# A first sum of activations moved from GpSimd to VectorE, and a norm's statistics from VectorE to ScalarE, in a streaming encoder step

## The chip, the cores and the metric

The kernel runs on one core of one Trainium2 chip. The metric is device time in microseconds (us) for one execution of the whole step, the median over repeated runs. Engines are named as in the profile: PE (TensorE matmul), PEld (its weight load), DVE (VectorE), ACT (ScalarE), POOL (GpSimd), SP (SyncE, which issues most DMAs).

## The reference

One layer is computed for 2048 prompt frames and 64 sample frames, D_MODEL = 1024, D_FF = 2816. The change lies in the last two lines of the layer, the SwiGLU and the last norm:

```
def _post(x, mix, ln1_g, ln1_b, w_gate_up, w_down, ln2_g, ln2_b):
    h = _layernorm(ALPHA * x + mix, ln1_g, ln1_b)
    gu = h @ w_gate_up
    f = (jax.nn.silu(gu[..., :D_FF]) * gu[..., D_FF:]) @ w_down
    return _layernorm(ALPHA * h + f, ln2_g, ln2_b)
```

## The kernel before

**Blocks and positions.** The frames are cut into four blocks b of 576, 512, 512 and 512 tokens; a block has four token tiles t of 128 rows (the first has a fifth of 64 rows). For each block the kernel goes over 22 slices i of 128 gate and up columns. The two matrix products of a slice are made by a seven-product scheme: products 1, 5, 6, 2, 7, 4, 3, each 12 fp32r matmuls of 256 columns (four pieces of K, three matmuls each for high and low parts, lines 909 to 911). `order` lists all products; the place of one in that list is its position. At each position the program writes the product, and then every step that was booked for that position with `at`. All queues run in the order in which the program is written; waits between engines are semaphores that follow from the data.

**Banks.** Products 1, 6, 7 and 4 of a slice add up one after another in the same PSUM bank A. Between them ScalarE copies the bank out (`keep`, line 915), and the next of them can't start before that copy. Product 2 has bank S1 (bankS in the profile), 5 and 3 bank C. VectorE adds the copies to other banks (lines 919, 946); ScalarE takes the silu (lines 950, 958).

**Chunks.** Two slices (2c and 2c+1) make a chunk c. In blocks 1 to 3, for chunks 2 to 9 (2 to 8 in block 3), which are 23 in all, the down product too is made by a seven-product scheme (`strassen`). There `out` multiplies silu and up into a tile g (line 926), two of them for a chunk (x and y in `f_sums`, each with two halves of 128x256), and `f_sums` makes four sums and differences of them on GpSimd at line 879, in the order of products 5, 7, 6, 3, in place. `put_hi` rounds such a sum on ScalarE (line 886, the high part) and `put_lo` subtracts that on VectorE (line 890, the low part). `unit(b, c, prod, u)` then makes one half of one product on PE: three matmuls of 512 columns at lines 1333, 1334, 1335, of which the third alone needs the low part; VectorE adds its bank to y (line 1338).

With p0 the position of product 3 of slice 2c+1, unit (5, 0) stands at p0 + 5, (6, 0) at p0 + 6; the high parts of 5, 6, 3, 7 at p0 + 3, 4, 5, 6 and the low parts one position later. The split of a gate/up weight slice, too, runs partly on GpSimd (line 113, wf<-guraw), and in some chunks GpSimd subtracts pieces of h for the next block (line 747, hsum and hraw).

**Where blocks meet.** The last chunk of a block ends within the first 20 positions of the next. For tile k of the block the two halves h of the down product stand at p0 + 10 + 2k and + 11 + 2k (line 1292 adds them to y), and the steps of `finish_steps` at + 2k + 11, 12, 13, 15, 17: statistics of half 0 (bn_stats, line 1354), of half 1 with mean and variance (line 1347) and 1/sqrt (line 91 and a small GpSimd instruction, line 92), gain (line 1367), shift (line 1371), store. In the first block all this is two positions later. There are 5 + 4 + 4 = 13 such tiles; the last block has its own ending, in which the statistics of three of its four tiles are already made from ScalarE's accumulated sums (`z_sum`, `z_mean`, `z_sq`, `z_var`, lines 1409 to 1425).

Of the kernel before, what the change touches and what calls it, by code (L numbers as in the profile page):

```python
# [16 lines left out]
P = 128  # L17
D = 1024
# [27 lines left out]
def hybrid_step(ctx: ExitStack, tc: tile.TileContext, x_prompt, x_sample, xT_prompt, xT_sample, cache_kT, cache_v, w_in,  # L46
# [824 lines left out]
        f = ffs[b, c, prod] = half_form()  # L871
        split(f[:, 0], f[:, 1], src)

    def f_sums(b, c):

        x, y = g_t.pop((b, 2 * c)), g_t.pop((b, 2 * c + 1))
        for prod, o, a, d, op in ((5, y[:, 1], x[:, 1], y[:, 1], ALU.add), (7, x[:, 1], x[:, 0], x[:, 1], ALU.subtract),
                                  (6, x[:, 0], y[:, 1], x[:, 0], ALU.subtract), (3, y[:, 0], y[:, 0], x[:, 0], ALU.subtract)):
            nc.gpsimd.tensor_tensor(out=o, in0=a, in1=d, op=op)
        for prod, o in ((5, y[:, 1]), (6, x[:, 0]), (7, x[:, 1]), (3, y[:, 0])):  # L880
            f_sum[b, c, prod] = o

    def put_hi(b, c, prod):

# [12 lines left out]
    def product(b, i, prod):  # L897
        n = TB[b] // 2
        w, h = wf.pop((b, i, prod)), forms[b, prod]
        bk = {1: "A", 6: "A", 7: "A", 4: "A", 2: "B", 5: "C", 3: "C"}[prod]  # L900
        new = prod in (1, 2, 5)
        if new:
            acc[i, bk] = (bank({"A": f"A{i % 2}", "C": f"C{i % 2}", "B": "S1"}[bk]) if b else
                          ps1.tile([P, 512], F32, name=f"acc{bk}", tag="x", bufs=6))
        ps = acc[i, bk][:, :n]
        for k in range(4):
            wh, wl, hh, hl = w[:, 0, k], w[:, 1, k], h[:, 0, k, :n], h[:, 1, k, :n]

            nc.tensor.matmul(ps, wh, hh, start=(new and k == 0), stop=False, skip_group_check=not new)  # L909
            nc.tensor.matmul(ps, wh, hl, start=False, stop=False, skip_group_check=not new)  # L910
            nc.tensor.matmul(ps, wl, hh, start=False, stop=(k == 3), skip_group_check=not new)  # L911

        def keep(key):
            part[i, key] = tmp(key)
            nc.scalar.copy(part[i, key][:, :n], ps)  # L915

        def add(key, to):
            part[i, key] = a = part.pop((i, to))
            nc.vector.tensor_tensor(out=a[:, :n], in0=ps, in1=a[:, :n], op=ALU.add)  # L919

        def out(sh, g, u):
            if strassen(b, i):
                if sh == 0:
                    g_t[b, i] = f2.tile([P, 4, P], F32, name="g", tag="wsum", bufs=3).rearrange("p (s a) q -> p s (a q)", s=2)
                to = g_t[b, i][:, sh]
                nc.vector.tensor_tensor(out=to, in0=u, in1=g, op=ALU.mult)

                if not (sh and i % 2 == 0):
                    put_f(b, i // 2, 4 if sh else 1 + i % 2, to)
                if sh and i % 2:  # L930
                    f_sums(b, i // 2)
                return
            nc.vector.tensor_tensor(out=g, in0=u, in1=g, op=ALU.mult)
            f = ff[b, i][:, :, sh * n:(sh + 1) * n] if b == 0 else half_form()
            if b:
                ff[b, i, sh] = f
            split(f[:, 0], f[:, 1], g)

        if prod == 1:
            keep("a0")  # L940
        elif prod == 6:
            keep("a1")
        elif prod == 7:
            keep("a2")
            part[i, "c22"] = a = part.pop((i, "a2"))
            nc.vector.tensor_tensor(out=a[:, :n], in0=acc[i, "C"][:, :n], in1=a[:, :n], op=ALU.add)
        elif prod == 2:
            add("c11", "a0")
            g = part[i, "c11"][:, :n]
            nc.scalar.activation(g, g, AF.Silu)  # L950
        elif prod == 4:
            if b == 0:
                ff[b, i] = f2.tile([P, 4 * NHX], F32R, name="ff", tag="ff", bufs=4)[:, :4 * n].rearrange("p (s t) -> p s t", s=2)
            out(0, part.pop((i, "c11"))[:, :n], ps)
        elif prod == 3:
            add("c12", "a1")
            g = part.pop((i, "c12"))[:, :n]
            nc.scalar.activation(g, g, AF.Silu)  # L958
            out(1, g, part.pop((i, "c22"))[:, :n])
# [399 lines left out]
    def finish_steps(t):  # L1359

        s_, m = {}, rows(t)

        def z(h):
            return y_t[t][:, h * 512:(h + 1) * 512]

        def gain():
            nc.vector.scalar_tensor_tensor(out=y_t[t][:m], in0=y_t[t][:m], scalar=s_["mv"][:m, 0:1], in1=ln2g[:m],
                                           op0=ALU.subtract, op1=ALU.mult)

        def shift():  # L1370
            nc.vector.scalar_tensor_tensor(out=y_t[t][:m], in0=y_t[t][:m], scalar=s_["rs"][:m, 0:1], in1=ln2b[:m],
                                           op0=ALU.mult, op1=ALU.add)

        def out():
            nc.sync.dma_start(out=y_out(t), in_=y_t.pop(t)[:m])

        return [lambda: stats(s_, (z(0), z(1)), m, 0), lambda: (stats(s_, (z(0), z(1)), m, 1), moments(s_, m)),
                gain, shift, out]


    zs, zp, zm = {}, {}, {}
# [71 lines left out]
    for b in range(NB):  # L1453
        first, last = b * NO, b == NB - 1
        for c in range(NFF // 2):
            p0 = start[b, 2 * c + 1, 3]
            d_load, d_split = (-8, -1, -5, -3), (-3, 5, -1, 4)
            if strassen(b, 2 * c):
                for prod, q0, q1 in ((1, -6, -3), (2, -5, -2), (5, -2, 2), (6, -1, 3), (3, 1, 5), (7, 4, 7), (4, 6, 9)):
                    at(p0 + q0, lambda b=b, c=c, prod=prod: load_f(b, c, prod))  # L1460
                    at(p0 + q1, lambda b=b, c=c, prod=prod: split_hi(b, c, prod))
                    at(p0 + q1 + 1, lambda b=b, c=c, prod=prod: split_lo(b, c, prod))
                for q, prod, u in ((0, 1, 0), (1, 2, 0), (2, 1, 1), (3, 2, 1), (5, 5, 0), (6, 6, 0), (7, 5, 1), (8, 3, 0), (8, 6, 1),
                                   (9, 3, 1), (10, 7, 0), (11, 7, 1), (12, 4, 0), (13, 4, 1)):
                    at(p0 + q, lambda b=b, c=c, prod=prod, u=u: unit(b, c, prod, u))
                for q, prod in ((3, 5), (4, 6), (5, 3), (6, 7)):
                    at(p0 + q, lambda b=b, c=c, prod=prod: put_hi(b, c, prod))
                    at(p0 + q + 1, lambda b=b, c=c, prod=prod: put_lo(b, c, prod))
                continue
# [25 lines left out]
            elif not last:  # L1495
# [4 lines left out]
                for k, t in enumerate(TILES[b]):  # L1500
                    for h in range(2):
                        at(p0 + 10 + 2 * k + (h if b else 2 - h), lambda b=b, c=c, t=t, h=h: down(b, c, t, h))
                    steps = finish_steps(t)
                    for q, f in zip((11, 12, 13, 15, 17), steps):
                        at(p0 + 2 * k + q + late, f)
                    at(p0 + 2 * k + 20 + late, lambda t=new.pop(0): new_y(t)) if new else None
        if not last:
# [106 lines left out]
```

## Time and profile before

| | us |
|---|---|
| median of 3 runs (2204.99 to 2209.4) | 2208.36 |
| the profiled execution, its own time | 2207.18 |
| its span, first to last instruction | 2205.4 |
| PE busy | 2089.7 (95%) |
| DVE busy | 1640.3 (74%) |
| ACT busy | 997.0 (45%) |
| POOL busy | 702.2 (32%) |

The profile is of one execution; a row of the time line gives an instruction's start in us from the span's start, its duration, engine, line, and in brackets how long the engine had been idle and who released it. A busy PE isn't a PE at its peak, so the reading goes by the places where PE is idle, and by who ended that idle time.

### The profile page before, as it was taken

The page shows a single profiled execution, that of the slowest core. Times are in us where ns is not written, and L with a number is a line of the kernel's source. Part 1 is how long each engine was busy: PE and PEld are TensorE (multiplying, and loading weights), DVE is VectorE, ACT ScalarE, POOL GpSimd, SP SyncE. Part 2 cuts the span into 40 slices and gives each one's busy share as a digit, 9 for nine tenths or more (in the row PEclk, how much of TensorE's full clock was granted, in tenths as well). Part 3 has the DMA queues.
Part 4 walks back from the last instruction along what each step waited for, and adds up shares of the span by engine and source line. Part 5 has one row for each costly group of instructions (what it writes and reads, how often), then busy time and mean ns, then how long its engine had stood idle before and what let it go on. Part 6 is the DMA issues. An engine that isn't in the chain of part 4 may idle for free.

```text
span 2205.4 us, 36220 instructions
## 1 busy us (share of the span) xinstructions
PE 2089.7 (95%) x13081; PEld 1861.6 (84%) x13081; DVE 1640.3 (74%) x3176; ACT 997.0 (45%) x2385; POOL 702.2 (32%) x644
## 2 busy tenths in 40 slices
PE   8999999989989899999999999999999999999997
PEld 6888888867768799999888888888888888988986
DVE  6877777786788677777786776777677778577775
ACT  6666666563343444444433443453343444344443
POOL 0222222231132567666531332222243222122221
PEclk9999999989999999999999999999999999999999
DMA  5111111043554866676776767787587777767663
GB/s 196 39 39 39 39 39 39 27 159 118 196 193 172 306 231 235 247 285 241 273 278 240 257 238 277 264 285 278 199 287 273 251 257 276 257 225 262 242 230 121
DMA packets 189156, 447.22 MB, mean 203 GB/s; under 512 B 22608, under 2 KB 53072, under 8 KB 188976
## 3 DMA queue, kind: packets, MB, share of 16 engines
q1 hardware_dynamic: 168432, 426.22, 54.9%
q10 hardware_dynamic: 20368, 18.35, 2.5%
q8 instruction: 103, 1.69, 0.3%
q14 instruction: 77, 0.63, 0.1%
q0 software_dynamic: 176, 0.33, 0.0%
HBM read 345.94 MB, written 98.89 MB: 202 GB/s over the span
## 4 chain that ended last, share of the span: by engine, by line
PE 65%; DVE 20%; ACT 6%; DMA 4%; issue 3%; POOL 1%; ACTq 0%; SPq 0%; DVEq 0%; POOLq 0%
PE bankA L909 5%; PE bankA L911 4%; PE bankA L910 4%; PE pj L158 2%; PE pj L159 2%; PE pj L160 2%; PE bankC L910 2%; PE bankC L909 2%; PE bankC L911 2%; PE pd L159 2%; PE pd L160 2%; PE pd L158 2%; PE bankD L1334 2%; PE bankD L1333 2%; PE bankD L1335 2%
## 5 line engine op out<-in xcount | busy, mean ns | idle before, releaser
L113 POOL TENSOR_TENSOR wf<-guraw,wf 128x512 fp32r<-128x512 f32 x173 | 245.7, 1420 | 626.9 <-ACT wf L112 598.4
L909 PE MATMUL bankA<-hf,wf 128*128 128x256 f32 x1056 | 301.8, 286 | 12.2 <-ACT a L915 11.9
L910 PE MATMUL bankA<-hf,wf 128*128 128x256 f32 x1056 | 300.1, 284 | 0.0
L911 PE MATMUL bankA<-hf,wf 128*128 128x256 f32 x1056 | 299.9, 284 | 0.0
L909 PEld LDWEIGHTS bankA<-hf,wf 128*128 128x128 f32 x1056 | 201.4, 191 | 22.7 <-ACT a L915 14.6
L910 PEld LDWEIGHTS bankA<-hf,wf 128*128 128x128 f32 x1056 | 201.2, 191 | 9.1
L911 PEld LDWEIGHTS bankA<-hf,wf 128*128 128x128 f32 x1056 | 201.4, 191 | 0.0
L112 ACT CAST wf<-guraw 128x512 fp32r<-128x512 f32 x264 | 163.1, 618 | 19.7 <-DMA guraw<-in_w_gate_up_dram 12.6
L915 ACT COPY a<-bankA 128x256 f32<-128x256 f32 x198 | 73.5, 371 | 174.8 <-PE bankA L911 174.4
L910 PE MATMUL bankC<-hf,wf 128*128 128x256 f32 x528 | 149.4, 283 | 2.6 <-DVE hf L113 2.6
L909 PE MATMUL bankC<-hf,wf 128*128 128x256 f32 x528 | 149.8, 284 | 0.9 <-DMA wf<-wf_d 0.8
L911 PE MATMUL bankC<-hf,wf 128*128 128x256 f32 x528 | 148.5, 281 | 0.0
L1338 DVE TENSOR_TENSOR y<-bankD,y 128x512 f32<-128x512 f32 x184 | 125.6, 683 | 30.5 <-PE bankD L1335 30.5
L1326 DVE TENSOR_TENSOR wd<-draw,wd 128x512 fp32r<-128x512 f32 x161 | 130.8, 813 | 0.0
L950 ACT ACTIVATE a<-a 128x256 f32<-128x256 f32 (+1 forms) x88 | 37.4, 425 | 200.7 <-DVE a L919 199.7
L909 PE MATMUL accA<-hf,wf 128*128 128x288 f32 x352 | 105.2, 299 | 8.9 <-ACT a L915 5.3
L958 ACT ACTIVATE a<-a 128x256 f32<-128x256 f32 (+1 forms) x88 | 37.4, 424 | 155.9 <-DVE a L919 155.8
L910 PEld LDWEIGHTS bankC<-hf,wf 128*128 128x128 f32 x528 | 99.5, 188 | 8.6 <-DVE hf L113 3.2
L1338 DVE TENSOR_TENSOR y<-bankS,y 128x512 f32<-128x512 f32 x138 | 94.4, 684 | 16.1 <-PE bankS L1335 13.7
L909 PEld LDWEIGHTS bankC<-hf,wf 128*128 128x128 f32 x528 | 99.8, 189 | 7.0 <-DMA wf<-wf_d 1.4
L911 PE MATMUL accA<-hf,wf 128*128 128x288 f32 x352 | 104.1, 296 | 0.4 <-DVE wf L113 0.4
L910 PE MATMUL accA<-hf,wf 128*128 128x288 f32 x352 | 104.4, 297 | 0.0
(336 smaller groups left out, 6712.1 us busy)
## 6 DMA issues: line engine op xcount, KB each, us to landing
wf<-wf_d SPq DMA_DIRECT2D x264, 512.0 KB, 4.9
guraw<-in_w_gate_up_dram SPq DMA_DIRECT2D x110, 512.0 KB, 6.2
wf_d<-wf SPq DMA_DIRECT2D x88, 512.0 KB, 4.9
draw<-in_w_down_dram SPq DMA_DIRECT2D x153, 256.0 KB, 3.5
draw<-wt_d SPq DMA_DIRECT2D x92, 256.0 KB, 4.3
guraw<-in_w_gate_up_dram SPq DMA_DIRECT2D x66, 256.0 KB, 6.4
wt_d<-draw SPq DMA_DIRECT2D x44, 256.0 KB, 3.3
hraw<-h_d SPq DMA_DIRECT2D x42, 256.0 KB, 4.7
```

What stands on the lines that cost most here:

```text
L112: nc.scalar.copy(hi, src)
L113: (on or nc.vector).tensor_tensor(out=lo, in0=src, in1=hi.bitcast(F32), op=ALU.subtract)
L158: nc.tensor.matmul(out, ah, bh, start=(i == 0), stop=False)
L159: nc.tensor.matmul(out, ah, bl, start=False, stop=False)
L160: nc.tensor.matmul(out, al, bh, start=False, stop=(i == n - 1))
L909: nc.tensor.matmul(ps, wh, hh, start=(new and k == 0), stop=False, skip_group_check=not new)
L910: nc.tensor.matmul(ps, wh, hl, start=False, stop=False, skip_group_check=not new)
L911: nc.tensor.matmul(ps, wl, hh, start=False, stop=(k == 3), skip_group_check=not new)
L915: nc.scalar.copy(part[i, key][:, :n], ps)
L1326: nc.vector.tensor_tensor(out=hl[:, 1], in0=d_raw.pop((b, c, "f", prod)), in1=hl[:, 0].bitcast(F32), op=ALU.subtract)
L1333: nc.tensor.matmul(pd, fh, w[:, 0], start=new, stop=False, skip_group_check=not new)
L1338: nc.vector.tensor_tensor(out=y, in0=pd, in1=y, op=ALU.add)
```

## The change

**In the 23 chunks**, the first sum of `f_sums` (that for product 5) is made on VectorE in `out`, right behind the multiplication that completes its inputs and ahead of the split of product 4. It goes into u, the buffer of the up half that was just read, in place of the tile's own half. GpSimd keeps three subtractions; the one for product 6 reads the new sum. The high part of 5 moves from p0 + 3 to p0 + 2, its low part from p0 + 4 to p0 + 3.

**Where blocks meet**, bn_stats and bn_aggr of 13 tiles go. ScalarE copies each half of y onto itself with an accumulated sum, VectorE makes minus the mean from the two sums, ScalarE squares y minus mean with an accumulated sum for each half, and VectorE makes the variance from these two. Variance and gain together stand at + 2k + 14, one position later than the gain stood; shift and store stay.

```
-    def f_sums(b, c):
+    def f_sums(b, c, first):
         x, y = g_t.pop((b, 2 * c)), g_t.pop((b, 2 * c + 1))
-        for prod, o, a, d, op in ((5, y[:, 1], x[:, 1], y[:, 1], ALU.add), (7, x[:, 1], x[:, 0], x[:, 1], ALU.subtract),
-                                  (6, x[:, 0], y[:, 1], x[:, 0], ALU.subtract), (3, y[:, 0], y[:, 0], x[:, 0], ALU.subtract)):
-            nc.gpsimd.tensor_tensor(out=o, in0=a, in1=d, op=op)
-        for prod, o in ((5, y[:, 1]), (6, x[:, 0]), (7, x[:, 1]), (3, y[:, 0])):
+        for prod, o, a, d in ((7, x[:, 1], x[:, 0], x[:, 1]), (6, x[:, 0], first, x[:, 0]), (3, y[:, 0], y[:, 0], x[:, 0])):
+            nc.gpsimd.tensor_tensor(out=o, in0=a, in1=d, op=ALU.subtract)
             f_sum[b, c, prod] = o
+        f_sum[b, c, 5] = first
...
                 nc.vector.tensor_tensor(out=to, in0=u, in1=g, op=ALU.mult)
+                if sh and i % 2:
+                    nc.vector.tensor_tensor(out=u, in0=g_t[b, i - 1][:, 1], in1=to, op=ALU.add)
...
                 if sh and i % 2:
-                    f_sums(b, i // 2)
+                    f_sums(b, i // 2, u)
...
+        def total(h):
+            if h == 0:
+                s_.update({x: f2.tile([P, 2], F32, name=f"y{x}", tag=f"z{x}", bufs=3) for x in ("sum", "sq", "mv", "rs")})
+            nc.scalar.activation(z(h)[:m], z(h)[:m], AF.Copy, accum_out=s_["sum"][:m, h:h + 1])
+        def squares():
+            nc.vector.tensor_scalar(s_["mv"][:m, 0:1], s_["sum"][:m, 0:1], s_["sum"][:m, 1:2], -1.0 / D, op0=ALU.add, op1=ALU.mult)
+            for h in range(2):
+                sq = f2.tile([P, 512], F32, name="zsq", tag="wsum", bufs=3)
+                nc.scalar.activation(sq[:m], z(h)[:m], AF.Square, bias=s_["mv"][:m, 0:1], accum_out=s_["sq"][:m, h:h + 1])
+        def variance():
+            nc.vector.tensor_scalar(s_["mv"][:m, 1:2], s_["sq"][:m, 0:1], s_["sq"][:m, 1:2], 1.0 / D, op0=ALU.add, op1=ALU.mult)
+            rstd(s_["rs"][:m, 0:1], s_["mv"][:m, 1:2], m, f2)
-        return [lambda: stats(s_, (z(0), z(1)), m, 0), lambda: (stats(s_, (z(0), z(1)), m, 1), moments(s_, m)),
-                gain, shift, out]
+        return [lambda: total(0), lambda: (total(1), squares()), lambda: (variance(), gain()), shift, out]
...
-                for q, prod in ((3, 5), (4, 6), (5, 3), (6, 7)):
+                for q, prod in ((2, 5), (4, 6), (5, 3), (6, 7)):
...
-                    for q, f in zip((11, 12, 13, 15, 17), steps):
+                    for q, f in zip((11, 12, 14, 15, 17), steps):
```

**The order on VectorE in a chunk.** Here is a piece of the first of the 23 chunks (block 1, chunk 2), before and with the change. L926/L925 writes g, L113 is a split's low part, L890/L889 is `put_lo`, L1338/L1340 adds a unit to y, L946/L948 waits for ScalarE's copy of product 7.

```order
L926 TENSOR_TENSOR g<-a_13189,a_13137 128x256
L113 TENSOR_TENSOR ff<-g,ff 128x256
L1338 TENSOR_TENSOR y<-bankD_12798,y 128x512
L113 TENSOR_TENSOR wf<-guraw,wf 128x512
L1338 TENSOR_TENSOR y<-bankS_12902,y 128x512
L1338 TENSOR_TENSOR y<-bankD_12852,y 128x512
L919 TENSOR_TENSOR a_13209<-bankS_12228,a_13209 128x256
L1326 TENSOR_TENSOR wd<-draw,wd 128x512
L1338 TENSOR_TENSOR y<-bankS_12902,y 128x512
L946 TENSOR_TENSOR a_13365<-bankC_12168,a_13365 128x256
L1326 TENSOR_TENSOR wd<-draw,wd 128x512
L890 TENSOR_TENSOR ff<-g,ff 128x256
```

With the change, the same stretch reads:

```order
L925 TENSOR_TENSOR g<-a_13219,a_13167 128x256
L928 TENSOR_TENSOR a_13219<-g 128x256
L113 TENSOR_TENSOR ff<-g,ff 128x256
L1340 TENSOR_TENSOR y<-bankD_12828,y 128x512
L113 TENSOR_TENSOR wf<-guraw,wf 128x512
L1340 TENSOR_TENSOR y<-bankS_12932,y 128x512
L1340 TENSOR_TENSOR y<-bankD_12882,y 128x512
L918 TENSOR_TENSOR a_13239<-bankS_12228,a_13239 128x256
L1328 TENSOR_TENSOR wd<-draw,wd 128x512
L1340 TENSOR_TENSOR y<-bankS_12932,y 128x512
L889 TENSOR_TENSOR ff<-a_13219,ff 128x256
L948 TENSOR_TENSOR a_13396<-bankC_12168,a_13396 128x256
```

The new sum (L928) stands behind the multiplication, and the low part of 5 has moved ahead of the addition that waits for product 7 and of a weight split.

**The order on ScalarE where blocks 1 and 2 meet**, at the copies of products 6 and 7 of slice 2 (L915/L914, out of bankA_12134). The two tiles whose statistics fall here are the block's last two. L950/L952 is the silu that waits for VectorE; L1383 is `total`, L1389 the squares, which wait for VectorE's mean.

```order
L915 COPY a_16546<-bankA_12134 128x256
L950 ACTIVATE a_16423<-a_16423 128x256
L112 CAST wd<-draw 128x512
L915 COPY a_16606<-bankA_12134 128x256
L112 CAST wf<-guraw 128x512
```

With the change, the same stretch reads:

```order
L914 COPY a_16590<-bankA_12134 128x256
L1383 ACTIVATE y,ysum<-y 128x512
L952 ACTIVATE a_16455<-a_16455 128x256
L1383 ACTIVATE y,ysum<-y 128x512
L1389 ACTIVATE zsq,ysq<-y,ymv 128x512 x2
L112 CAST wd<-draw 128x512
L914 COPY a_16656<-bankA_12134 128x256
```

Between the silu and the copy of product 7, which product 4 waits for, there are now one `total` and two squares.

## Rows read from the trace of the kernel before

**Rows 1.** The waits of PE over the whole span: who waited for whom, us in total, times, longest.

```profile
PE bankS L1335 <- DVE ff L890: 25.3, 23, 2.2
PE bankA L909 <- ACT a L915: 11.9, 5, 4.7
```

**Rows 2.** The time line of PE around unit (5, 0) and unit (6, 0) of block 1, chunk 2 (start, duration, engine, line).

```profile
1224.23 0.39 PE L1333 MATMUL bankS<-wd,ff 128*128 128x512 f32 x1
1224.46 0.40 PE L1334 MATMUL bankS<-wd,ff 128*128 128x512 f32 x1
1225.91 0.50 PE L1335 MATMUL bankS<-wd,ff 128*128 128x512 f32 x1 [1.05 <-DVE ff L890]
1226.25 0.28 PE L909 MATMUL bankA<-hf,wf 128*128 128x256 f32 x1
...
1228.16 0.40 PE L1335 MATMUL bankD<-wd,ff 128*128 128x512 f32 x1
```

**Rows 3.** The time line of DVE in the same chunk.

```profile
1215.80 0.43 DVE L926 TENSOR_TENSOR g<-a,a 128x256 f32<-128x256 f32 x1 [0.48 <-ACT a L958]
1216.70 0.42 DVE L113 TENSOR_TENSOR ff<-g,ff 128x256 fp32r<-128x256 f32 x1 [0.47 <-ACT ff L112]
...
1220.89 0.42 DVE L919 TENSOR_TENSOR a<-bankS,a 128x256 f32<-128x256 f32 x1 [0.73 <-PE bankS L911]
...
1221.83 0.68 DVE L1338 TENSOR_TENSOR y<-bankS,y 128x512 f32<-128x512 f32 x1
...
1224.36 1.50 DVE L890 TENSOR_TENSOR ff<-g,ff 128x256 fp32r<-128x256 f32 x1
...
1227.06 0.41 DVE L890 TENSOR_TENSOR ff<-g,ff 128x256 fp32r<-128x256 f32 x1
```

**Rows 4.** The time line of POOL: the four sums of that chunk and the weight split behind them, and a subtraction of h in chunk 3.

```profile
1217.21 3.51 POOL L879 TENSOR_TENSOR g<-g 128x256 f32<-128x256 f32 x4 [2.77 <-DVE ff L113]
1224.29 1.29 POOL L113 TENSOR_TENSOR wf<-guraw,wf 128x512 fp32r<-128x512 f32 x1 [3.58 <-ACT wf L112]
...
1256.62 1.48 POOL L747 TENSOR_TENSOR hsum<-hraw,hsum 128x512 f32<-128x512 f32 x1
```

**Rows 5.** The time line of ACT in chunk 2: the last work at position p0 + 2, and the high part of 5.

```profile
1219.03 0.62 ACT L1322 CAST wd<-draw 128x512 fp32r<-128x512 f32 x1
...
1222.18 0.40 ACT L886 CAST ff<-g 128x256 fp32r<-128x256 f32 x1
```

**Rows 6.** The time line of PE at five more of its stalls: behind the meeting of blocks 0 and 1, at unit (5, 0) of chunk 3 in block 1, behind the meeting of blocks 1 and 2, at unit (5, 0) of chunk 5 in block 2, and behind the meeting of blocks 2 and 3.

```profile
1165.90 0.39 PE L909 MATMUL bankA<-hf,wf 128*128 128x256 f32 x1 [4.71 <-ACT a L915]
...
1257.01 0.51 PE L1335 MATMUL bankS<-wd,ff 128*128 128x512 f32 x1 [1.05 <-DVE ff L890]
...
1517.42 0.39 PE L909 MATMUL bankA<-hf,wf 128*128 128x256 f32 x1 [2.84 <-ACT a L915]
...
1681.46 0.50 PE L1335 MATMUL bankS<-wd,ff 128*128 128x512 f32 x1 [2.16 <-DVE ff L890]
...
1873.92 0.58 PE L909 MATMUL bankA<-hf,wf 128*128 128x256 f32 x1 [2.84 <-ACT a L915]
```

**Rows 7.** Four stretches: start and end, length, busy us (instructions) of PE, PEld, DVE, ACT, POOL, then the granted TensorE clock (1.00 is full speed), DMA share and GB/s.

```profile
1166.46:1169.87 3.41, 3.41 (x18) 3.41 (x17) 3.41 (x5) 0.00 (x0) 0.58 (x1) 0.50 0.23 92
1518.04:1521.45 3.41, 3.41 (x15) 3.02 (x14) 3.41 (x3) 0.12 (x1) 2.45 (x2) 0.50 1.03 422
1681.88:1685.29 3.41, 3.41 (x16) 3.22 (x15) 1.45 (x3) 0.62 (x3) 0.67 (x1) 0.50 1.04 422
1873.02:1879.85 6.83, 5.93 (x22) 5.35 (x22) 6.29 (x10) 3.06 (x8) 3.17 (x2) 0.50 1.00 385
```

**Rows 8.** The time line of DVE where blocks 1 and 2 meet.

```profile
1511.23 0.21 DVE L1347 BATCH_NORM_AGGREGATE ymv<-yst 128x2 f32<-128x12 f32 x1
1511.48 0.15 DVE L91 TENSOR_SCALAR rs_e<-ymv 128x1 f32<-128x1 f32 x1
...
1513.34 1.28 DVE L1367 SCALAR_TENSOR_TENSOR y<-y,ymv,ln2g 128x1024 f32<-128x1024 f32 x1
1514.54 0.68 DVE L1292 TENSOR_TENSOR y<-bankS,y 128x512 f32<-128x512 f32 x1
1515.14 0.68 DVE L1354 BATCH_NORM_STATS2 yst<-y 128x6 f32<-128x512 f32 x1
1515.74 0.41 DVE L919 TENSOR_TENSOR a<-bankS,a 128x256 f32<-128x256 f32 x1
```

**Rows 9.** The time line of ACT at the same place.

```profile
1516.18 0.42 ACT L950 ACTIVATE a<-a 128x256 f32<-128x256 f32 x1 [6.90 <-DVE a L919]
...
1517.01 0.36 ACT L915 COPY a<-bankA 128x256 f32<-128x256 f32 x1
```

**Rows 10.** The time lines of ACT and of DVE in the kernel's ending, where the last block's statistics are made from accumulated sums.

```profile
2180.83 0.63 ACT L1409 ACTIVATE y<-y 128x512 f32<-128x512 f32 x1 [1.09 <-DVE y L1393]
...
2182.45 0.72 ACT L1420 ACTIVATE zsq<-y,zmv 128x512 f32<-128x512 f32 x1 [0.28 <-DVE zmv L1414]
...
2184.01 0.21 DVE L1425 TENSOR_SCALAR zmv<-zsq 128x1 f32<-128x1 f32 x1 [1.59 <-ACT zsq L1420]
...
2187.05 0.21 DVE L1414 TENSOR_SCALAR zmv<-zsum 128x1 f32<-128x1 f32 x1
```

More of the change, by code (lines that the diff above doesn't have):

```diff
@@ L1367, in gain @@
             nc.vector.scalar_tensor_tensor(out=y_t[t][:m], in0=y_t[t][:m], scalar=s_["mv"][:m, 0:1], in1=ln2g[:m],
-                                           op0=ALU.subtract, op1=ALU.mult)
+                                           op0=ALU.add, op1=ALU.mult)
         def shift():
```

## Prediction

> **What bounds the kernel now.** I read the table of busy times first: PE is busy for 95% of the span, so only what ends PE's idle time can move the end. The waits of PE come next [rows 1]. The largest by far is one line, the third matmul of a unit (L1335), which waits 23 times, 25.3 us in all, for the low part that `put_lo` makes on VectorE (L890). 23 is the number of the chunks that the change touches. The second is PE waiting for ScalarE's copy out of bank A (L915). The time line shows where that second wait is large: three times, for 4.71, 2.84 and 2.84 us, just behind the meeting of two blocks [rows 6].
>
> Why the low part is late shows when PE, VectorE, GpSimd and ScalarE are laid beside each other in one chunk. Unit (5, 0) starts at 1224.23, its second matmul at 1224.46, and the third is due 0.23 later, at 1224.69; it starts at 1225.91 [rows 2]. VectorE begins the low part at 1224.36 and needs 1.50 us for it, though the same instruction takes 0.41 at 1227.06 [rows 3]. In between GpSimd runs a weight split, from 1224.29 to 1225.58 [rows 4], and the low part ends 0.28 after that split. So it isn't the sum on GpSimd that comes too late, it is done at 1220.72 [rows 4]; the high part on ScalarE is done at 1222.58 [rows 5]. The low part is written so late that it meets the split.
>
> **The chunks, part by part.** *Removed wait.* With the change the low part of 5 stands directly behind the addition of 1221.83 [rows 3], whose successor would start near 1222.5. Its inputs: the new sum, made right behind the multiplication of 1215.80, that is by about 1216.6 [rows 3]; and the high part, now behind the cast of 1219.03, so near 1220.1 [rows 5]. It ends near 1222.9, 1.8 us before PE wants it, and GpSimd is idle until 1224.29 [rows 4]. So the stall goes whole. Its worth is more than the 1.05 of idle time: the third matmul is 1.22 late, and the next product starts 0.34 behind it where 0.24 is usual, together 1.32 [rows 2]. The 25.3 us are 22 stalls of 1.05 and one of 2.16 [rows 1, 6]. The one of 2.16 is followed by 3.41 us at a granted clock of 0.50, which is 1.2 GHz [rows 7]; work at half speed loses half of it, 1.7. The sum is 22 x 1.32 + (2.16 + 0.27 + 1.7) = 29.0 + 4.1 = 33.1 us.
>
> *Added work.* One addition of 128x256 on VectorE, at most 0.43 by the multiplication beside it. VectorE is idle for 0.47 at that very place, since the low part of product 4 waits for its cast [rows 3]; the addition fits into that gap, so it costs nothing. Without that cover it would be 23 x 0.43 = 10 us of VectorE's time, still ahead of an idle 0.73 at 1220.89 [rows 3]. The cast of 5 moves into time in which ScalarE waits for the silu's input; 0.40 there is covered too [rows 5].
>
> *What collides anew.* GpSimd used to wait for the low part of product 4; now it may start its first subtraction as soon as the addition ends, beside that low part, which has two inputs in SBUF like L890. A subtraction is about 0.88 (3.51 for four [rows 4]), so that low part can be held for up to 0.88. Nobody needs it before p0 + 12, and VectorE's 0.73 of idle time takes up most of it [rows 3]. I take zero.
>
> *What is late next.* The low part of 6 starts 1.15 behind the third matmul of unit (5, 0), and is due 2.25 behind it (1225.91, 1227.06, 1228.16 [rows 2, 3]). Once the stall is gone this becomes 1224.69 + 1.15 = 1225.84, 0.26 behind the end of GpSimd's split [rows 4]: free, but narrowly. In chunk 3 it isn't: the third matmul moves from 1257.01 to 1255.79, the low part would start at 1256.94, in the subtraction of h of 1256.62 to 1258.10, and end 0.28 behind it at 1258.38; due at 1258.04, so 0.34 come back [rows 4, 6]. Chunk 3 is there twice: 0.7. Chunk 5, in which GpSimd has more such subtractions, also twice: no row shows it without its stall; between nothing and the whole 1.32 I take 1.32 each, 2.6, since the row of 2.16 shows the more crowded case [rows 6]. Net gain of the chunks: 33.1 - 3.3 = 29.8 us.
>
> **The meetings, part by part.** VectorE is the late one there. Its silu input (L919) comes at 1515.74, ScalarE has been idle for 6.90 us waiting for it, the copy of product 7 follows at 1517.01, and PE goes on at 1517.42 [rows 6, 8, 9]. *Removed* per tile: two bn_stats of 0.60 and a bn_aggr of 0.25, by the starts that follow each other, 1.45 [rows 8]. *Added* on VectorE: two instructions of 0.21 [rows 10]. So VectorE gains 1.03 a tile, and by the booked positions the statistics of tiles 1 and 2 and half of tile 3's stand between the start of the backlog and that L919: it can come 2.6 earlier.
>
> *The added wait.* The copy now stands behind a `total` and two squares, and the squares wait for a mean that VectorE makes behind variance and gain. Before, the copy started 1.27 behind L919, in which the weight cast took about 0.41 [rows 8, 9]. Now: L919 0.41, variance 0.21, the step to 1/sqrt 0.15, gain 1.20, mean 0.21, two squares of 0.72, the cast 0.41: 4.03, so 2.8 later [rows 8, 10]. Queued behind the waiting square are exactly the copies that PE waits for. That is 0.2 lost at this place, and at the third meeting, which is built alike. The first has a fifth tile, so four tiles' relief (4.1) stands against about the same path: 1.3 better. I take 1 us gained for all three, with the half-clock stretches kept. The ends: all three stalls gone, 4.71 + 2.84 + 2.84 = 10.4, and with them 3.41 + 3.41 + 6.83 at half clock, 6.8 [rows 6, 7]: 17.2 gained; or no relief reaches L919, because VectorE itself waits for casts behind the squares: 3 x 2.8 = 8.4 lost.
>
> **The sum** against the profiled execution: 2207.18 - 29.8 - 1 = 2176.4. The median of the runs before lies 1.2 above it, so **2177.6**.
>
> **A rule weighed.** Rows 3 and 4 show a two-input VectorE instruction held beside a GpSimd subtraction, 1.50 instead of 0.41. The Trainium skill, GPSIMD Engine Reference, section 1 (Specifications), says that GpSimd shares its SBUF interfaces with VectorE, with contention for VectorE instructions that have two SBUF inputs. It speaks against this change, which adds one such instruction and moves GpSimd's work; by it alone the hold would move to whichever low part is next, and that result is the third rival below.
>
> **The rivals.** (1) *The meetings come free*: VectorE's relief is used in full, and the squares run while PE has other work. For it: ScalarE is idle for 6.90 us there [rows 9]. Against it: the path of 4.03. Time: 2177.6 - 16.2 = 2161. (2) *The meetings get worse* by 8.4: 2177.6 + 1 + 8.4 = 2187. (3) *The hold moves to the low part of 6 in every chunk*: the margin is 0.26, the price 0.34 as in chunk 3: 2177.6 + 21 x 0.34 = 2185. (4) *The change doesn't do what it says*: the low part of 5 is held by another GpSimd instruction or waits for its cast, and the whole stall stays; 2208.4 - 1 = 2207. (5) *Slower*: one round trip of the new statistics, from the first accumulated sum to the variance, is 3.18 us in the ending (2180.83 to 2184.01 [rows 10]); if it came onto PE's path for each of the 13 tiles, it would be 41 us, and 2177.6 + 1 + 41 = 2220. It decides from ten tiles on (29.8 / 3.18). Against it: VectorE's gain and shift of the neighbouring tile lie beside it.
>
> **How the numbers follow.** Chances: the forecast 0.55, (1) 0.15, (2) 0.10, (3) 0.11, (4) 0.05, (5) 0.04. The predicted time is the forecast's, 2177.6. The range reaches to (1) below and past each of (2) and (3) above, short of both together (2194): 2160 to 2192; it leaves out (4), (5) and parts of (1). A difference of 0.2% (4.4 us) is about what a measurement can tell from no change: (4), at 2207, counts as the same, 0.05; slower is (5), 0.04; faster 0.91.
>
> **What would show it.** Right: PE's wait for the low part at L1335 falls from 25.3 us to under 4, the low part of 5 takes 0.41 and is done before unit (5, 0), VectorE's new addition takes about 0.43, and a chunk gets shorter by 1.3. At the meetings bn_stats is gone and the waits for the copies (L915 before, L914 after) stay near 2 to 4.5 us, now behind squares. Wrong: a new wait of unit (6, 0) in every chunk (3), stalls behind the meetings that vanish (1) or pass 5 us (2, 5), or a low part of 5 that still takes 1.5 us (4).

## The result, and the profile after

| | before | after |
|---|---|---|
| median, us | 2208.51 (2204.99 to 2209.4, 4 runs) | 2184.39 (2181.52 to 2184.76, 4 runs) |
| ratio, 95% interval | | 0.9891 (0.9874 to 0.9908) |
| profiled execution, its own time | 2207.18 | 2181.52 |
| its span | 2205.4 | 2179.4 |
| PE / DVE / ACT / POOL busy | 2089.7 / 1640.3 / 997.0 / 702.2 | 2085.4 / 1611.9 / 1032.2 / 698.2 |

The kernel is 1.1% faster. The forecast, 2177.6, was 6.8 us too low, and the range of 2160 to 2192 holds the result. Of the ten executions of e2 below, one ran at a granted clock of 0.556 and took 3383.44 us; its ratio is made without that one. Line numbers move by a few: the third matmul of a unit is L1337 now (L1335 before), the low part L889, the copies L914, the first matmul of a product's trio L908.

The waits of PE over the whole span come first, as in [rows 1].

```profile
PE bankA L908 <- ACT a L914: 14.6, 7, 5.0
PE bankS L908 <- DVE y L1340: 8.7, 7, 2.3
...
PE bankD L1337 <- DVE ff L889: 1.0, 3, 0.7
```

The line with 25.3 us is gone: no third matmul of unit (5, 0) waits any more. What is left of waits for a low part, 1.0 us, belongs to unit (6, 0). The wait for ScalarE's copies grew from 11.9 to 14.6.

**In a chunk.** The time line of PE in block 1, chunk 2, where [rows 2] stand before:

```profile
1223.83 0.39 PE L1335 MATMUL bankS<-wd,ff 128*128 128x512 f32 x1
1224.06 0.40 PE L1336 MATMUL bankS<-wd,ff 128*128 128x512 f32 x1
1224.29 0.39 PE L1337 MATMUL bankS<-wd,ff 128*128 128x512 f32 x1
1224.53 0.28 PE L908 MATMUL bankA<-hf,wf 128*128 128x256 f32 x1
...
1226.43 0.40 PE L1337 MATMUL bankD<-wd,ff 128*128 128x512 f32 x1
```

The three matmuls follow each other 0.23 apart and the next product 0.24 behind. DVE in the same chunk, against [rows 3]:

```profile
1215.40 0.43 DVE L925 TENSOR_TENSOR g<-a,a 128x256 f32<-128x256 f32 x1 [0.48 <-ACT a L960]
1215.86 0.42 DVE L928 TENSOR_TENSOR a<-g 128x256 f32<-128x256 f32 x1
1216.30 0.42 DVE L113 TENSOR_TENSOR ff<-g,ff 128x256 fp32r<-128x256 f32 x1
...
1221.42 0.68 DVE L1340 TENSOR_TENSOR y<-bankS,y 128x512 f32<-128x512 f32 x1
1222.03 0.41 DVE L889 TENSOR_TENSOR ff<-a,ff 128x256 fp32r<-128x256 f32 x1
...
1224.72 0.69 DVE L1340 TENSOR_TENSOR y<-bankS,y 128x512 f32<-128x512 f32 x1 [0.68 <-PE bankS L1337]
1225.33 0.42 DVE L889 TENSOR_TENSOR ff<-g,ff 128x256 fp32r<-128x256 f32 x1
```

POOL there, against [rows 4]:

```profile
1216.37 0.96 POOL L878 TENSOR_TENSOR g<-g 128x256 f32<-128x256 f32 x1 [2.33 <-DVE a L928]
...
1223.89 1.30 POOL L113 TENSOR_TENSOR wf<-guraw,wf 128x512 fp32r<-128x512 f32 x1 [4.54 <-ACT wf L112]
```

And ACT, against [rows 5]:

```profile
1218.63 0.62 ACT L1324 CAST wd<-draw 128x512 fp32r<-128x512 f32 x1
1219.15 0.41 ACT L885 CAST ff<-a 128x256 fp32r<-128x256 f32 x1
```

The new sum (L928) sits in the gap of 0.47 that stood ahead of the low part of product 4; that low part follows without a gap and isn't held (0.42): it starts 0.07 ahead of GpSimd's subtraction (1216.30 against 1216.37), and so it does in all 23 chunks. The low part of 5 ends at 1222.44, 1.45 before GpSimd's split begins at 1223.89, and takes 0.41 where it took 1.50. The low part of 6 starts at 1225.33, 0.14 behind the end of that split. In 21 of the 23 chunks the low part of 5 takes 0.41 or 0.42; in chunk 5 of blocks 1 and 2 it starts beside a GpSimd instruction and takes 0.92 and 0.91, without a wait of PE.

**Where blocks meet.** The time line of PE at its stalls, against [rows 6]: the first meeting, unit (6, 0) of chunk 5 in block 1, and two stalls each at the second and third meeting. The row of 1506.71 is no stall: it is product 4's first matmul at the second meeting, behind product 7 and, in the other bank A, product 1 of the next slice, which the program makes between the two.

```profile
1164.93 0.58 PE L908 MATMUL bankA<-hf,wf 128*128 128x256 f32 x1 [5.03 <-ACT a L914]
...
1317.65 0.50 PE L1337 MATMUL bankD<-wd,ff 128*128 128x512 f32 x1 [0.67 <-DVE ff L889]
...
1501.42 0.58 PE L908 MATMUL bankA<-hf,wf 128*128 128x256 f32 x1 [2.73 <-ACT a L914]
...
1506.71 0.41 PE L908 MATMUL bankA<-hf,wf 128*128 128x256 f32 x1
...
1518.48 0.39 PE L908 MATMUL bankA<-hf,wf 128*128 128x256 f32 x1 [1.22 <-ACT a L914]
...
1852.78 0.58 PE L908 MATMUL bankA<-hf,wf 128*128 128x256 f32 x1 [2.73 <-ACT a L914]
...
1869.84 0.39 PE L908 MATMUL bankA<-hf,wf 128*128 128x256 f32 x1 [1.96 <-ACT a L914]
```

The granted clock (the 0.50 ahead of the last two columns), by the same windows as in [rows 7]: the three meetings, and chunk 5 of block 2 in third place.

```profile
1162.90:1169.73 6.83, 4.80 (x22) 4.80 (x23) 5.47 (x8) 3.24 (x9) 1.46 (x1) 0.50 0.41 160
1500.80:1507.63 6.83, 6.21 (x29) 6.21 (x30) 4.70 (x10) 5.41 (x16) 2.31 (x2) 0.50 1.03 377
1678.30:1681.72 3.42, 3.42 (x16) 3.13 (x15) 2.11 (x4) 0.42 (x1) 0.00 (x0) 0.50 0.87 298
1852.40:1855.81 3.41, 3.03 (x14) 3.03 (x15) 2.83 (x7) 2.49 (x8) 1.52 (x1) 0.50 1.03 358
```

DVE at the second meeting, against [rows 8]. L1392 is the variance, L91 and L1369 the step to 1/sqrt and the gain, L1386 the mean, L918 (L919 before) the silu's input, L1373 the shift; L935 (L933 before) is a multiplication that waits for a silu.

```profile
1492.74 1.29 DVE L935 TENSOR_TENSOR a<-a,a 128x256 f32<-128x256 f32 x1 [1.49 <-ACT a L960]
...
1497.84 0.21 DVE L1392 TENSOR_SCALAR ymv<-ysq 128x1 f32<-128x1 f32 x1
1498.09 0.15 DVE L91 TENSOR_SCALAR rs_e<-ymv 128x1 f32<-128x1 f32 x1
1498.16 1.27 DVE L1369 SCALAR_TENSOR_TENSOR y<-y,ymv,ln2g 128x1024 f32<-128x1024 f32 x1
1499.35 0.21 DVE L1386 TENSOR_SCALAR ymv<-ysum 128x1 f32<-128x1 f32 x1
...
1501.87 0.41 DVE L918 TENSOR_TENSOR a<-bankS,a 128x256 f32<-128x256 f32 x1
...
1506.00 0.69 DVE L113 TENSOR_TENSOR wd<-draw,wd 128x512 fp32r<-128x512 f32 x1 [2.09 <-ACT wd L112]
...
1506.94 2.26 DVE L1373 SCALAR_TENSOR_TENSOR y<-y,yrs,ln2b 128x1024 f32<-128x1024 f32 x1
```

Of the multiplication, the row before was:

```profile
1504.16 0.76 DVE L933 TENSOR_TENSOR a<-a,a 128x256 f32<-128x256 f32 x1 [0.48 <-ACT a L958]
```

ACT there, against [rows 9]; L1389 is a square.

```profile
1499.59 0.72 ACT L1389 ACTIVATE zsq<-y,ymv 128x512 f32<-128x512 f32 x1 [2.11 <-DVE ymv L1386]
...
1500.31 0.70 ACT L1389 ACTIVATE zsq<-y,ymv 128x512 f32<-128x512 f32 x1
...
1501.02 0.35 ACT L914 COPY a<-bankA 128x256 f32<-128x256 f32 x1
...
1505.36 0.60 ACT L112 CAST wd<-draw 128x512 fp32r<-128x512 f32 x1
1505.87 0.36 ACT L914 COPY a<-bankA 128x256 f32<-128x256 f32 x1
```

Before, PE stood 2.84 us ahead of product 4, for the copy of product 7. Now it stands 2.73 us ahead of product 7, for the copy of product 6 (1501.02). That copy is queued behind two squares, and these waited 2.11 for the mean, which VectorE made behind variance and gain of the tile before. Later the weight cast (1505.36) stands behind the next two squares, VectorE waits 2.09 for it, and a shift that takes 1.27 elsewhere takes 2.26 beside a GpSimd split (before, a gain took 2.31 there, at 1519.27, so that this is not new). A second stall of 1.22 follows at 1518.48. Over the three meetings (1130 to 1900 us) ScalarE's wait for the mean is this one row of its waits (us in total, times, longest):

```profile
ACT zsq L1389 <- DVE ymv L1386: 15.5, 13, 2.3
```

**Where the 26 us lie.** The same PE instruction in both traces, at the borders of the stretches, in us from the span's start:

| up to | before | after | ahead by | gained in the stretch |
|---|---|---|---|---|
| ahead of the first meeting | 1147.07 | 1146.11 | 0.96 | 0.96 |
| behind it | 1207.79 | 1207.38 | 0.41 | -0.55 |
| end of the chunks of block 1 | 1502.91 | 1489.88 | 13.03 | 12.62 |
| behind the second meeting | 1552.66 | 1541.79 | 10.87 | -2.16 |
| end of the chunks of block 2 | 1852.17 | 1834.02 | 18.15 | 7.28 |
| behind the third meeting | 1901.93 | 1885.26 | 16.67 | -1.48 |
| end of the chunks of block 3 | 2143.52 | 2117.68 | 25.84 | 9.17 |

The chunks gain 29.1 us in all, the three meetings lose 4.2. The table compares one execution with one. By the same comparison the meetings of the experiments below that leave them as before stand at -1.3 (e1), -0.2 (e3), 0.4 (e4) and 0.0 (e5), and those of e2, which has only the meetings' part, at -4.5; the chunks gain 30.2 in e1 and 27.3 in e3. So differences of that size in it mean little; the meetings' loss is clear of them.

### The profile page after: what moved, and what is told of

Read it like the earlier page. It is cut to its first block, busy times and chain, and to the rows that moved or that the text cites. A ratio compares the mean times of both kernels' runs of the same rounds, so it can differ in the third digit from the quotient of the medians.

```text
span 2179.4 us, 36315 instructions
## 1 busy us (share of the span) xinstructions
PE 2085.4 (96%) x13081; PEld 1864.2 (86%) x13081; DVE 1611.9 (74%) x3186; ACT 1032.2 (47%) x2489; POOL 698.2 (32%) x621
## 3 DMA queue, kind: packets, MB, share of 16 engines
q8 instruction: 103, 1.69, 0.3%
## 4 chain that ended last, share of the span: by engine, by line
PE 69%; DVE 18%; ACT 5%; DMA 3%; issue 3%; POOL 1%; ACTq 0%; SPq 0%; DVEq 0%; POOLq 0%
PE bankA L908 5%; PE bankA L909 5%; PE bankA L910 5%; PE pj L158 3%; PE pj L159 3%; PE pj L160 3%; PE bankC L908 2%; PE bankC L909 2%; PE bankC L910 2%; PE pd L159 2%; PE pd L160 2%; PE pd L158 2%; PE po L158 2%; PE po L160 2%; PE po L159 2%
## 5 line engine op out<-in xcount | busy, mean ns | idle before, releaser
L113 POOL TENSOR_TENSOR wf<-guraw,wf 128x512 fp32r<-128x512 f32 x173 | 242.0, 1399 | 653.7 <-ACT wf L112 631.1
L908 PE MATMUL bankA<-hf,wf 128*128 128x256 f32 x1056 | 302.7, 287 | 14.7 <-ACT a L914 14.6
L908 PEld LDWEIGHTS bankA<-hf,wf 128*128 128x128 f32 x1056 | 202.7, 192 | 26.9 <-ACT a L914 17.7
L914 ACT COPY a<-bankA 128x256 f32<-128x256 f32 x198 | 73.5, 371 | 166.5 <-PE bankA L910 166.0
L908 PE MATMUL bankC<-hf,wf 128*128 128x256 f32 x528 | 149.5, 283 | 0.5 <-DMA wf<-wf_d 0.5
L1340 DVE TENSOR_TENSOR y<-bankD,y 128x512 f32<-128x512 f32 x184 | 125.8, 684 | 30.0 <-PE bankD L1337 29.9
L952 ACT ACTIVATE a<-a 128x256 f32<-128x256 f32 (+1 forms) x88 | 37.4, 425 | 176.4 <-DVE a L918 175.4
L908 PE MATMUL accA<-hf,wf 128*128 128x288 f32 x352 | 105.0, 298 | 8.5 <-ACT a L914 4.9
L1340 DVE TENSOR_TENSOR y<-bankS,y 128x512 f32<-128x512 f32 x138 | 94.6, 686 | 16.8 <-PE bankS L1337 14.4
L908 PEld LDWEIGHTS bankC<-hf,wf 128*128 128x128 f32 x528 | 99.5, 188 | 6.3 <-DMA wf<-wf_d 1.0
```

The costliest lines, as they stand in the source:

```text
L113: (on or nc.vector).tensor_tensor(out=lo, in0=src, in1=hi.bitcast(F32), op=ALU.subtract)
L1340: nc.vector.tensor_tensor(out=y, in0=pd, in1=y, op=ALU.add)
```

## The experiments

The question was first whether the chunks' gain comes from the re-timing, from the sum's new engine or from GpSimd's split, and whether the meetings lose; then what they lose it to. All times are medians; ratios are to the kernel before on the same chip.

**e1_chunks_only** and **e2_meetings_only** take the change apart: the kernel after with `finish_steps` and its positions of before, and the kernel before with the new `finish_steps` and positions.

```diff
-        return [lambda: total(0), lambda: (total(1), squares()), lambda: (variance(), gain()), shift, out]
+        return [lambda: stats(s_, (z(0), z(1)), m, 0), lambda: (stats(s_, (z(0), z(1)), m, 1), moments(s_, m)), gain, shift, out]
-                    for q, f in zip((11, 12, 14, 15, 17), steps):
+                    for q, f in zip((11, 12, 13, 15, 17), steps):
```

This is e1 against the kernel after, shortened to the lines that decide, with the list of the steps on one line; the new functions and the gain's sign go with it. e2 against the kernel before has the same lines the other way round, and the new functions.

> The chunk part of the change alone, with the block meetings as they were. Theory (the chunks give some 29 us, the meetings take some 4 of them back): about 2179 us, PE's wait at the third matmul of unit (5, 0) gone in all 23 chunks, stalls behind the meetings as before (4.7, 2.8, 2.8 us). Rival (the shortfall against the forecast arose in the chunks, by a new hold or wait there): about 2184, like the whole change.

> The part of the change at the block meetings alone, chunks as before. Theory (the copies that PE waits for stand behind squares that wait for VectorE's mean): 2 to 6 us slower than before, 2210 to 2215, with stalls of 3 to 5 us behind each meeting. Rival (the meetings gained about 1 us, and the loss comes only when both parts are together): 2206 to 2208.

e1: 2180.5 us, ratio 0.9875 (0.9857 to 0.9893). e2: 2213.57 us, ratio 1.0027 (1.0018 to 1.0037). In e1 no third matmul of unit (5, 0) waits, and the longest stalls behind the meetings are those of before (4.71, 2.84, 2.85). By the medians the chunks alone give more than the whole change (the intervals overlap); the meetings alone cost 0.27%, some 6 us. In e2 the second and third meeting lose 2.1 and 1.5 us by the same comparison as above, as in the kernel after. Its waits of PE show both facts, the stalls of the chunks kept and the copies' wait raised from 11.9 to 14.6:

```profile
PE bankS L1335 <- DVE ff L890: 25.8, 23, 2.2
PE bankA L909 <- ACT a L915: 14.6, 7, 5.1
```

**e3_move_only** and **e4_sum_only** part the two halves of the chunks' edit, both against the kernel before. In e3 GpSimd keeps the sum and only the cast and low part move up:

```diff
-                for q, prod in ((3, 5), (4, 6), (5, 3), (6, 7)):
+                for q, prod in ((2, 5), (4, 6), (5, 3), (6, 7)):
```

In e4 VectorE makes the sum, as in the change, and nothing moves:

```diff
+                    nc.vector.tensor_tensor(out=u, in0=g_t[b, i - 1][:, 1], in1=to, op=ALU.add)
...
-                    f_sums(b, i // 2)
+                    f_sums(b, i // 2, u)
```

> Only the booked position of product 5's high and low part is moved one earlier; all four sums stay on GpSimd, the meetings as before. Theory (the low part was late only because it was written where GpSimd's weight split holds it; the sum on GpSimd is done in time): the whole gain of the chunks, about 2179. Rival (the sum has to come from VectorE at once): the low part waits for GpSimd's sum or its cast, and at most half of the 29 us comes, 2193 or above.

> Only the first sum goes to VectorE; product 5's high and low part stay at their old positions, the meetings as before. Theory: the low part still meets the weight split and takes 1.5 us, the stall of 1.05 stays 23 times, 2206 to 2210. Rival (the engine of the sum decides): 2179 to 2190.

e3: 2181.09 us, ratio 0.9879 (0.9864 to 0.9894), the same as e1 within the intervals: one number in a table gives the gain of the chunks, and the sum may stay on GpSimd. e4: 2205.2 us, ratio 0.9988 (0.9978 to 0.9998), a tenth of a per cent, just below what was expected: all 23 stalls stay. The low part of 5 in e4, in the view of one line (minimum, median and maximum in ns, first and last start), is as slow as before in each of the 23 chunks:

```profile
L889 DVE TENSOR_TENSOR ff<-a,ff x23: 1479/1501/1502, 1225.2 to 2124.7; 128x256 fp32r<-128x256 f32 x23
```

**e5_split_off_gpsimd** leaves order and sums as before and moves only the split that ran beside the low part, that of product 2's weights, from GpSimd to VectorE in these chunks.

```diff
-        split(f[:, 0], f[:, 1], src, nc.gpsimd if prod in (1, 2) and made > EARLY else None)
+        split(f[:, 0], f[:, 1], src, nc.gpsimd if prod in (1, 2) and made > EARLY and not (prod == 2 and i % 2 and strassen(b, i - 2)) else None)
```

> The kernel before, with nothing moved but one weight split per chunk (product 2 of the odd slices, the one that stands beside the low part of 5) from GpSimd to VectorE. Theory (the low part takes 1.50 us because GpSimd runs beside it): at its old place it takes 0.41, ends near 1224.77 where 1224.69 is due, the stall falls from 1.05 to under 0.2 in most of the 23 chunks, and the time to 2180 to 2188 (VectorE has 0.6 more per chunk). Rival (the low part is slow or late for another reason, its cast or its input): stall and 1.50 stay, 2206 to 2212.

2185.75 us, ratio 0.9891 (0.9875 to 0.9908). The low part is no earlier, but it takes 0.41 or 0.42 in 21 of the 23 chunks, where 23 took 1.48 to 1.50. In chunk 2, the first row here, PE doesn't wait. Four stalls of unit (5, 0) are left of 23 (0.57, 2.17, 0.57 and 1.69 us), in chunks 3 and 5 of blocks 1 and 2, the chunks in which GpSimd subtracts pieces of h (in chunk 5 it still takes 1.48):

```profile
1226.76 0.42 DVE L890 TENSOR_TENSOR ff<-g,ff 128x256 fp32r<-128x256 f32 x1
...
1257.85 0.50 PE L1335 MATMUL bankS<-wd,ff 128*128 128x512 f32 x1 [0.57 <-DVE ff L890]
...
1320.69 0.50 PE L1335 MATMUL bankS<-wd,ff 128*128 128x512 f32 x1 [2.17 <-DVE ff L890]
```

So the hold beside GpSimd was the cause of the stalls, and there are two cures: to write the low part earlier (e3) or to take the split away (e5).

**e6_squares_later** and **e7_gain_earlier** change where the meetings' new steps stand, both against the kernel after. e6 makes the squares a step of their own, one position behind the mean, and with that behind the copy:

```diff
-        return [lambda: total(0), lambda: (total(1), squares()), lambda: (variance(), gain()), shift, out]
+        return [lambda: total(0), lambda: (total(1), mean()), squares, lambda: (variance(), gain()), shift, out]
-                    for q, f in zip((11, 12, 14, 15, 17), steps):
+                    for q, f in zip((11, 12, 13, 14, 15, 17), steps):
```

e7 writes variance and gain one position earlier, so that they stand a position ahead of the next tile's mean instead of at the same one:

```diff
-                    for q, f in zip((11, 12, 14, 15, 17), steps):
+                    for q, f in zip((11, 12, 13, 15, 17), steps):
```

> The changed kernel, with the two squares of the meetings booked one position behind the mean, so that ScalarE comes to them when the mean is there. Theory (the copy that PE waits for stands behind a square that waits for the mean): ScalarE's waits for the mean shrink from 2.1 to under 0.5, the stalls behind the meetings fall from 5.0, 2.7 and 2.7 to at most half, 2176 to 2181. Rival (VectorE's load, or ScalarE's added 2.9 us of work a tile, decides): stalls as in the changed kernel, 2183 to 2187.

> The changed kernel, with variance and gain one position earlier (where the gain stood before), so that the next tile's mean doesn't stand behind them. Theory: ScalarE's squares wait 1.4 us less for the mean, but VectorE comes to the variance sooner and may wait for the squares; 2179 to 2184. Rival (gain's place doesn't matter): 2184 or above.

e6: 2176.26 us, ratio 0.9853 (0.9836 to 0.9869), the fastest kernel here; its interval ends just below that of the kernel after. The meetings now gain 4.2 us against the kernel before (0.6, 1.5 and 2.1). At the second meeting the copy of product 6 (1499.66) now stands ahead of the squares (1501.60), and PE doesn't wait for it. ScalarE's wait for the mean falls from 15.5 us in 13 to 4.9 in 4, the longest still 1.6 where under 0.5 was expected. The stalls are 4.42 at the first meeting and, at the second, these:

```profile
1506.18 0.39 PE L908 MATMUL bankA<-hf,wf 128*128 128x256 f32 x1 [1.15 <-ACT a L914]
...
1518.28 0.39 PE L908 MATMUL bankA<-hf,wf 128*128 128x256 f32 x1 [1.89 <-ACT a L914]
```

The stalls were expected to halve at least; over the three meetings they fall from 14.1 us (5.03, 2.73, 1.22, 2.73, 0.42, 1.96) to 10.5 (4.42, 1.15, 1.89, 1.16, 1.84), which is 3.6 of the 8.4 us that the meetings differ by. The rest goes with the clock, which in this trace stays full through the second and third meeting:

```profile
1505.00:1522.00 17.00, 13.96 (x101) 12.94 (x101) 14.26 (x22) 9.11 (x23) 6.15 (x5) 1.00 0.99 369
1850.00:1867.00 17.00, 14.13 (x100) 13.10 (x101) 14.10 (x22) 8.95 (x23) 6.14 (x5) 1.00 1.01 374
```

The profiled execution is one of four; their mean granted clocks run from 0.985 (2179.6 us) to 0.988 (2173.5), those of the kernel after from 0.984 (2184.76) to 0.986 (2184.19). So part of the distance of the medians is the clock, and why it falls less often in e6 isn't shown.

e7: 2185.73 us, ratio 0.9894 (0.988 to 0.9909), no gain over the kernel after, against what was expected. The squares' wait halves, to 7.6 us, but VectorE now waits for ScalarE's sums, 4.5 us in 9 waits, one of which is

```profile
1509.94 0.21 DVE L1386 TENSOR_SCALAR ymv<-ysum 128x1 f32<-128x1 f32 x1 [1.10 <-ACT y L1383]
```

and the copies still stand behind the squares (stalls of 5.87 at the first meeting, 1.53 and 2.94 at the second). The rival's range held. Of the two, only the order on ScalarE's own queue helps.

**e8_last_tile_bn** is e6 with bn_stats again for the last tile of each block, **e9_squares_twice** the kernel after with every square made twice, the second over the first.

e8 against e6, shortened to the lines that decide (the gain's sign goes with them), with the list on one line:

```diff
+        by_bn = t in [tiles[-1] for tiles in TILES]
...
+        if by_bn:
+            return [lambda: stats(s_, (z(0), z(1)), m, 0), lambda: (stats(s_, (z(0), z(1)), m, 1), moments(s_, m)), lambda: None, gain, shift, out]
```

e9, a line that `squares` then has twice:

```diff
+                nc.scalar.activation(sq[:m], z(h)[:m], AF.Square, bias=s_["mv"][:m, 0:1], accum_out=s_["sq"][:m, h:h + 1])
```

> As the run with the squares one position later, but the last tile of each block takes its statistics on VectorE by bn_stats again, as before the change. Theory (what is left behind the first meeting, 4.42 us, is the copy standing behind the last tile's squares, which wait for the mean behind a gain): the first stall falls to 2 to 3 us and the time by 1 to 3 us, to 2173 to 2175. Rival (VectorE's load decides there): the stall stays at 4.4 or grows by VectorE's added 1.0 us, 2176 to 2179.

> The changed kernel with each square of the meetings made twice in a row (the same result), 1.4 us more on ScalarE for each of the 13 tiles and nothing added on VectorE. Theory (the copy behind the squares is on PE's path): the stalls of 2.73 behind the second and third meeting grow by 1.2 to 1.6 each, that of 5.03 behind the first likewise, 2187 to 2192. Rival (VectorE's work is on PE's path, ScalarE has slack): stalls within 0.4 of the changed kernel's, 2183 to 2186.

e8: 2179.47 us, ratio 0.9869 (0.985 to 0.9888), about 3 us above e6, though the intervals overlap; neither theory's time held. The first meeting's stall falls from 4.42 to 1.40, with a new one of 1.77 behind it (1170.81), while the second meeting's later stall grows from 1.89 to 3.16 (1518.26). The work of one tile, given back to VectorE, takes a stall away at one copy and makes another longer; that both engines are near their limit there is a reading of it, not shown. e9: 2201.69 us, ratio 0.9968 (0.9956 to 0.9979), 17 us above the kernel after. The main stalls grow by 4.8, 3.4 and 3.4 (the third, at 1872.30, is as long as the second), where two squares more were to add 1.2 to 1.6:

```profile
1175.31 0.58 PE L908 MATMUL bankA<-hf,wf 128*128 128x256 f32 x1 [9.82 <-ACT a L914]
...
1517.46 0.58 PE L908 MATMUL bankA<-hf,wf 128*128 128x256 f32 x1 [6.13 <-ACT a L914]
```

ScalarE's squares are thus on PE's path. That a delay grows on its way round, ScalarE to VectorE and back, is a reading of this excess that no run isolates.

## Why the prediction was right, and where it was off

**The stall of the chunks: right in mechanism and size.** The hold beside the split, not a late sum, was the step on which everything rested. e4 (sum moved, stall kept), e3 (sum kept, stall gone) and e5 (split moved, stall gone) bear it out. The Trainium skill, GPSIMD Engine Reference, section 1 (Specifications), says that GpSimd contends with VectorE's instructions of two SBUF inputs; the traces agree (1.50 beside the split, 0.42 without it in e5). Its rule as a rival, the hold on the low part of 6 in every chunk, didn't come: that one starts 0.14 behind the split instead of the 0.26 worked out, and is free. 29.8 us net were predicted, 29.1 measured. The chunks without pieces of h gain 1.28 to 1.34 each in the traces, 1.32 as worked out.

**Chunks 3 and 5: right only in sum.** Chunk 3 was to give back 0.34, by a hold of the low part of 6. That hold came (1.39 us), PE waits 0.18 for it (block 1, 1256.55), and the chunk gains 0.88 and 0.85 in the two blocks, some 0.45 less than the others. Chunk 5 was taken as a net of 0 in block 1 and 2.8 gained in block 2. PE's instructions at 1315.12 and 1339.56 before stand at 1311.16 and 1331.83 after, 3.8 gained; those at 1677.13 and 1698.11 stand at 1662.76 and 1684.74, 1.0 lost. The two errors cancel, which is luck. A stretch at half clock is gone from chunk 5 of block 1, and one stayed in block 2 (1678.30), behind waits for VectorE's addition of a unit and not for a low part.

**The added work: zero, right.** The sum takes 0.42 in the gap of 0.47; the low part of product 4 beside GpSimd's first subtraction takes 0.42, where up to 0.88 of hold had been allowed. Zero was taken because nobody needs that low part early; in the trace it isn't held at all, as it starts first.

**The meetings: the mis-sized term.** 1 us gained was predicted, 4.2 lost were measured. The path from L919 to the copy of product 7 was sized rightly: 4.03 predicted, 1505.87 - 1501.87 = 4.00 measured. But no stall stands behind it: held before product 7 and then at half clock, PE comes to product 4 only at 1506.71, behind the end of that copy (1506.23). Two things were wrong beside it. VectorE's relief: L918 was to come 2.6 earlier; it comes at 1501.87 instead of 1515.74 in a program that is 13.03 ahead by then, so 0.84 earlier. Of the 1.76 that are missing, 1.01 is VectorE's longer wait for a silu (1.49 at 1492.74, 0.48 before), which is queued behind two squares on ScalarE, and 0.53 the multiplication behind that wait, 1.29 for 0.76, both beside a GpSimd split. The forecast had let VectorE's relief reach L919 whole; that VectorE itself could wait behind squares stood only in its bad end and in rival (2). And the step "queued behind the waiting square are exactly the copies that PE waits for" was applied to one copy only. The squares of the tile before stand ahead of the copy of product 6, which PE had not waited for before; that one costs 2.73, and the prediction's path begins behind it. The backlog then goes on, through VectorE's wait of 2.09 for a cast behind squares, to a second stall; that chain is read from the rows, and no run takes out this wait alone. Rival (2) had this direction and this cause, VectorE waiting behind squares, with 8.4; half of that came, and the first stall, 5.03, just passes the 5 us that were to be its sign. e6, which changes only the squares' place on ScalarE, turns the loss into a gain, and so shows the order there to be the cause; how much of that gain is the clock's own, one trace doesn't tell.

**The rest.** Of the 6.8 us, the meetings are 5.2, the chunks 0.7. Against that 1.1 were gained outside both, 0.96 of it ahead of the first meeting, where no instruction was changed; the medians' distance from the profiled executions, 2.9 after and 1.2 before, makes most of what remains.

## What to carry to other kernels

When VectorE and GpSimd share work, look at what runs beside each short VectorE instruction on PE's path: here one position earlier in the order was worth 27 us (2208.49 to 2181.09), and where the sum was made was worth some 3 (2205.2). When statistics move to ScalarE, write the instruction that waits for another engine behind the copies that free PSUM, and follow each copy in its queue, also those that were never late. A relief on one engine is worth only what reaches the next wait of PE.

## What the runs showed of the hardware

**Which VectorE instructions are held.** Beside the same GpSimd split (1223.89 to 1225.19 in the kernel after) the addition that reads a PSUM bank, L1340 at 1224.72, takes 0.69; without one, at 1221.42, 0.68. The instructions seen longer beside GpSimd read SBUF alone: L890 1.50 for 0.41, the shift L1373 2.26 for 1.27. They are held, not slowed: every low part of the 23 chunks that starts within a GpSimd instruction of L113 or L747 (45 in the kernel before, 27 after) ends 0.28 to 0.29 behind the end of that instruction, wherever in it it started. The low part of product 4, which after the change starts 0.06 to 0.07 ahead of GpSimd's subtraction, takes 0.42 or 0.43 in all 23 chunks and isn't held.

**The clock.** A stall of PE was sometimes followed by a stretch of 3.41 us at half clock, sometimes by a longer one, sometimes by none, at the same idle time. In the kernel before, waits of 2.25 (at 1462.42) and 2.26 (at 1819.38) were followed by

```profile
1463.42:1466.83 3.41, 3.41 (x15) 3.12 (x15) 2.90 (x6) 1.44 (x3) 0.00 (x0) 0.50 1.01 387
1819.38:1822.80 3.42, 3.42 (x25) 3.28 (x26) 3.32 (x7) 1.12 (x3) 0.00 (x0) 1.00 0.95 346
```

The first meeting's stall of 4.71 was followed by 3.41 us at half clock before and by 6.83 in e1 (1168.60 to 1175.43). Such stretches move single chunks by one or two us either way; what decides between them stays open.
